# Seven block products in place of eight for the gate and up projections of layer 1

## The chip, the cores and the metric

The kernel runs on one core of one Trainium2 chip. The metric is the time of one execution on the device in microseconds; three executions of the kernel before are known. One execution was also taken by the hardware profiler, and all rows below are from its trace.

## What is computed

The reference is a two-layer backbone over 512 latent tokens of width 1024, with 256 context tokens beside them. Each layer mixes tokens (four groups of heads) and then applies a feed-forward network (FFN) to each token:

```python
def swiglu(h, w_in_, w_out_):
    gate, up = jnp.split(h @ w_in_, 2, axis=-1)
    return (jax.nn.silu(gate) * up) @ w_out_

x = x + g_a * rms_norm(mix_x @ w_out, norm_g[1])
x = x + g_f * rms_norm(swiglu(modulate(rms_norm(x, norm_g[2]), sh_f, sc_f), w_ffn_in, w_ffn_out), norm_g[3])
```

The hidden layer of the FFN has 2816 columns, that is 22 tiles of 128, once for gate and once for up. The second layer, which the code counts as l = 1, has an FFN for the latent tokens only. It is the last thing that the kernel does.

## The kernel before, in words

Every matrix is held transposed: features in the 128 partitions, tokens along the columns. A tile has 128 features, so h (1024 features, 512 tokens) is eight tiles `hf0` to `hf7`. Products are made from float32 numbers that are split into a rounded part `hi` and a remainder `lo`, and each product of tiles is three matmuls (hi by hi, lo by hi, hi by lo; lines 425 to 427). The weights come from DRAM in units of 512 KB (L380, tiles `wr`, four buffers) and are split when they arrive: ACT writes `hi` (L366, tiles `wh`, five buffers of 128x512), and `lo` = source minus `hi` is made on POOL or DVE (L367, tiles `wl`, four buffers). PSUM results of PE are in tiles `mm`, of which there are four.

The end of a layer (`layer_end`) is the output projection, the residual and the norm of the FFN's input (`modnorm`, lines 518 to 533: a product on DVE in L525, `hi` on ACT in L527, `lo` on POOL or DVE), both for one half of the tokens and then for the other, and then `ffn`. In layer 1 `ffn` takes the 22 hidden tiles in three chunks of 8, 7 and 7. The first three tiles run in halves of 256 tokens while the second half's norm is still being made. For each of the other 19 tiles, a unit of gate weights and a unit of up weights arrive, and 48 matmuls of 512 columns (8 tiles of rows, three matmuls each, twice) give two PSUM tiles. `ffn_gate` (lines 1452 to 1460) makes the hidden tile of them:

```python
nc.scalar.activation(a, pg, AF.Tanh)                                                                        # L1456
nc.vector.scalar_tensor_tensor(out=a, in0=a, scalar=1.0, in1=pg, op0=ALU.add, op1=ALU.mult)                  # L1457
nc.vector.tensor_tensor(out=a, in0=pu, in1=a, op=ALU.mult)                                                   # L1458
self.split(g.h[j], g.l[j], a, scale=0.5)   # ACT L369, DVE L370
```

After each chunk come eight output products, one for each tile of features of y, over the chunk's hidden tiles (`ffo`). They are copied or added into y by ACT (L1404) or DVE (L1406). The last chunk's products end in halves, and then the residual is made and stored.

No order is written by hand: the tile framework's scheduler sets it from its own estimates, and each engine then runs its instructions strictly in that order. An instruction that waits for a buffer or an operand therefore holds all that stand behind it on its engine.

## Time and profile before

| | before |
|---|---|
| three executions | 1692.64, 1692.86, 1695.9 us |
| median | 1692.86 us |
| profiled execution: span from first to last instruction | 1692.6 us |
| mean granted TensorE clock in it | 0.972 |
| busy: PE | 1624.3 us (96%) |
| busy: DVE, ACT, POOL | 944.4 us (56%), 740.5 us (44%), 607.2 us (36%) |
| DMA moved | 215.10 MB, 126 GB/s read from HBM over the span |
| chain that ended last | PE 83%, DVE 8%, DMA 3%, ACT 2%, POOL 1% |

PE is TensorE's matmuls, DVE is VectorE, ACT ScalarE, POOL GpSimd and SP the engine that issues the loads. Busy time is the time in which an instruction ran or was held while running; the chain that ended last is the work followed back from the last instruction through whatever released it. The profiled execution's own time is the span, which lies 0.3 us under the median, so a sum made against the profile needs no correction. Layer 1's FFN is the last stage: its norm begins at about 1303 us, its 19 whole hidden tiles and their output products fill the time from about 1346 us on.

### The profile page before, as it was taken

The page shows a single profiled execution, that of the slowest core. Times are in us where ns is not written, and L with a number is a line of the kernel's source. Part 1 is how long each engine was busy: PE and PEld are TensorE (multiplying, and loading weights), DVE is VectorE, ACT ScalarE, POOL GpSimd, SP SyncE. Part 2 cuts the span into 40 slices and gives each one's busy share as a digit, 9 for nine tenths or more (in the row PEclk, how much of TensorE's full clock was granted, in tenths as well). Part 3 has the DMA queues.
Part 4 walks back from the last instruction along what each step waited for, and adds up shares of the span by engine and source line. Part 5 has one row for each costly group of instructions (what it writes and reads, how often), then busy time and mean ns, then how long its engine had stood idle before and what let it go on. Part 6 is the DMA issues. An engine that isn't in the chain of part 4 may idle for free.

```text
span 1692.6 us, 27131 instructions
## 1 busy us (share of the span) xinstructions
PE 1624.3 (96%) x9935; PEld 1381.3 (82%) x9935; DVE 944.4 (56%) x2172; ACT 740.5 (44%) x1658; POOL 607.2 (36%) x691
## 2 busy tenths in 40 slices
PE   6899999999999999999999998999798999999997
PEld 2876778787989998888888888999578988888887
DVE  4876675858685569542443466758765531232344
ACT  3654456654445655333332334465565433332331
POOL 2421333664466565322222225332425322222233
PEclk9999999999999998999999998999799999999998
DMA  9554564254466423334334452122042122323221
GB/s 315 178 181 154 190 222 125 98 176 129 148 230 184 148 74 116 112 138 149 138 127 150 137 201 95 59 73 70 2 132 81 38 93 94 98 82 107 92 95 51
DMA packets 81045, 215.10 MB, mean 127 GB/s; under 512 B 10512, under 2 KB 18576, under 8 KB 80912
## 3 DMA queue, kind: packets, MB, share of 16 engines
q1 hardware_dynamic: 80912, 213.37, 38.3%
q8 instruction: 78, 1.28, 0.3%
q14 instruction: 55, 0.45, 0.1%
HBM read 209.14 MB, written 4.19 MB: 126 GB/s over the span
## 4 chain that ended last, share of the span: by engine, by line
PE 83%; DVE 8%; DMA 3%; issue 2%; ACT 2%; POOL 1%; SPq 0%; DVEq 0%; POOLq 0%; ACTq 0%
PE mm L425 22%; PE mm L427 22%; PE mm L426 22%; PE ms L584 2%; PE mx L1097 2%; PE mm L437 1%; PE mx L1091 1%; PE mm L438 1%; DMA wm_m<-in_wmod_dram 1%; PE mx L1349 1%; PE mm L449 1%; PE mm L443 1%; PE mm L442 1%; PE mm L444 1%; DVE wl L367 1%
## 5 line engine op out<-in xcount | busy, mean ns | idle before, releaser
L366 ACT ACTIVATE wh<-wr 128x512 fp32r<-128x512 f32 (+3 forms) x526 | 318.9, 616 | 581.5 <-PE mm L426 478.9
L367 POOL TENSOR_TENSOR wl<-wr,wh 128x512 fp32r<-128x512 f32 (+2 forms) x248 | 322.8, 1304 | 666.1 <-PE mm L427 517.8
L367 DVE TENSOR_TENSOR wl<-wr,wh 128x512 fp32r<-128x512 f32 (+3 forms) x278 | 206.7, 747 | 180.5 <-PE mm L427 131.5
L425 PE MATMUL mm<-hfh_m,wh 128*128 128x512 f32 (+1 forms) x656 | 253.7, 387 | 0.0
L426 PE MATMUL mm<-hfl_m,wh 128*128 128x512 f32 (+1 forms) x656 | 253.5, 386 | 0.0
L427 PE MATMUL mm<-hfh_m,wl 128*128 128x512 f32 (+1 forms) x656 | 253.4, 386 | 0.0
L425 PEld LDWEIGHTS mm<-hfh_m,wh 128*128 128x128 f32 x656 | 123.7, 188 | 26.5
L427 PEld LDWEIGHTS mm<-hfh_m,wl 128*128 128x128 f32 x656 | 123.5, 188 | 26.5
L426 PEld LDWEIGHTS mm<-hfl_m,wh 128*128 128x128 f32 x656 | 123.5, 188 | 26.5
L425 PE MATMUL mm<-gh_m,wh 128*128 128x512 f32 x275 | 108.3, 394 | 0.0
L426 PE MATMUL mm<-gl_m,wh 128*128 128x512 f32 x275 | 108.1, 394 | 0.0
L427 PE MATMUL mm<-gh_m,wl 128*128 128x512 f32 x275 | 108.0, 393 | 0.0
L1458 DVE TENSOR_TENSOR ft_m<-mm,ft_m 128x512 f32<-128x512 f32 (+1 forms) x50 | 31.3, 626 | 133.2 <-PE mm L427 131.7
L426 PE MATMUL mm<-hfl_c,wh 128*128 128x256 f32 x352 | 100.3, 285 | 1.0 <-POOL hfl_c L532 1.0
L425 PE MATMUL mm<-hfh_c,wh 128*128 128x256 f32 x352 | 99.9, 285 | 0.0
L427 PE MATMUL mm<-hfh_c,wl 128*128 128x256 f32 x352 | 99.2, 283 | 0.0
L627 DVE SCALAR_TENSOR_TENSOR macc_m<-wr,cs,macc_m 128x512 f32<-128x512 f32 x56 | 44.1, 787 | 65.8 <-DMA wr<-in_wmod_dram 64.8
L425 PEld LDWEIGHTS mm<-hfh_c,wh 128*128 128x128 f32 x352 | 66.2, 188 | 4.0 <-issue 3.4
L426 PEld LDWEIGHTS mm<-hfl_c,wh 128*128 128x128 f32 x352 | 66.3, 188 | 2.3 <-POOL hfl_c L532 1.2
L427 PEld LDWEIGHTS mm<-hfh_c,wl 128*128 128x128 f32 x352 | 66.1, 188 | 1.3 <-issue 1.0
L1406 DVE TENSOR_TENSOR y_m<-mm,y_m 128x256 f32<-128x256 f32 (+1 forms) x43 | 23.6, 551 | 68.2 <-PE mm L427 68.2
L427 PEld LDWEIGHTS mm<-gh_m,wl 128*128 128x128 f32 x275 | 51.7, 188 | 12.0
(597 smaller groups left out, 4165.5 us busy)
## 6 DMA issues: line engine op xcount, KB each, us to landing
wr<-in_wfi_dram SPq DMA_DIRECT2D x132, 512.0 KB, 3.6
wr<-in_wmod_dram SPq DMA_DIRECT2D x80, 512.0 KB, 3.6
wr<-in_wT_dram SPq DMA_DIRECT2D x42, 512.0 KB, 3.8
wr<-in_wfo_dram SPq DMA_DIRECT2D x32, 512.0 KB, 3.5
wr<-in_wfo_dram SPq DMA_DIRECT2D x32, 448.0 KB, 3.3
wr<-in_wo_dram SPq DMA_DIRECT2D x24, 512.0 KB, 3.6
wm_m<-in_wmod_dram SPq DMA_DIRECT2D x32, 256.0 KB, 5.3
wr<-in_wRB_dram SPq DMA_DIRECT2D x12, 384.0 KB, 3.3
```

The source lines that it names most:

```text
L366: nc.scalar.activation(hi, src, AF.Copy)
L367: (eng or nc.vector).tensor_tensor(out=lo, in0=src, in1=hi.bitcast(F32), op=ALU.subtract)
L425: nc.tensor.matmul(out, lh, rh, start=first, stop=False)
L426: nc.tensor.matmul(out, lh, rl, start=False, stop=False)
L427: nc.tensor.matmul(out, ll, rh, start=False, stop=last)
L437: nc.tensor.matmul(out, w.h[w0 + i], ah, start=f, stop=False)
L438: nc.tensor.matmul(out, w.l[w0 + i], ah, start=False, stop=False)
L584: nc.tensor.matmul(ps[o:o + 32, :], self.cs[:, k, :], ws[i], start=True, stop=True, tile_position=(0, o))
L627: nc.vector.scalar_tensor_tensor(out=t, in0=w, scalar=self.cs[:, k, s:s + 1], in1=t, op0=ALU.mult, op1=ALU.add)
L1097: nc.tensor.matmul(po[kv * 64:kv * 64 + 64, 0:256], stream.av.t[b][:, kv * 64:kv * 64 + 64], pts[kv].t[:, i * 256:(i + 1) * 256], start=i0 ...
L1406: nc.vector.tensor_tensor(out=yt, in0=ps, in1=yt, op=ALU.add)
L1458: nc.vector.tensor_tensor(out=a, in0=pu, in1=a, op=ALU.mult)
```

## The change

For the 19 whole hidden tiles of layer 1, gate and up are computed as one product of 2x2 blocks in Strassen's form (Winograd's variant). The rows of the pair of block matrices are gate and up, the sum over 1024 features is cut into two halves of four tiles, and the tokens into two halves of 256. The product then takes seven products of blocks and a number of sums in place of eight products of blocks.

- `Quarters` holds h as four blocks `hf00`, `hf01`, `hf10`, `hf11`, and a float32 copy, `keep`. With `keep`, `modnorm` has one more ACT operation for those tiles of features whose `lo` was made on DVE, and `lo` is a plain difference.
- `strassen_rhs` makes four sums of blocks of h, `st0` to `st3`, once: 16 differences on 128x256, 16 `hi` on ACT and 16 `lo`; half of the differences and of the `lo` are on POOL, half on DVE.
- `strassen_pair` replaces the dense products and `ffn_gate` for each of the 19 tiles. It adds four sums of weights (`s[0]` and `s[2]` on POOL, `s[1]` and `s[3]` on DVE, tiles `ws`, four buffers), splits seven blocks of 128x512 (products 0, 3, 4 and 6 with `lo` on POOL, 1, 2 and 5 on DVE), makes 7 x 4 x 3 = 84 matmuls of 256 columns, and takes partial sums out of PSUM between the products.
- The chunks of hidden tiles are 4, 4, 4, 3 and 7 in place of 8, 7 and 7, so there are 40 output products in place of 24 with the same number of matmuls, each with its copy or sum into y, and 40 loads of output weights in place of 24, of the same total size.
- One unit less is loaded ahead for the FFN (`preu1` 3 in place of 4), and the program's scratch for dynamic DMAs is given a size.

```diff
- 'preu1': 4,
+ 'preu1': 3,
...
+ 'strassen': (1,),
+ 'fcs': ((0, 4), (4, 8), (8, 12), (12, 15), (15, 22)),
+ 'sad': 'PPVV',
+ 'slo': 'PVVPPVP',
+ 'sup': 'V',
+ 'sgl': 'V',
+ 'ws': 4}
...
+            if keep is not None:
+                nc.scalar.activation(keep.t[k], tt, AF.Identity, bias=B[:, k:k + 1])
+                self.e(T["mnk"][k]).tensor_tensor(out=lo, in0=keep.t[k], in1=hi.bitcast(F32), op=ALU.subtract)
+            elif T["mnk"][k] == "V":
...
+    def strassen_rhs(self, h):
...
+        sub = lambda c, o, a, b: self.e(c).tensor_tensor(out=o, in0=a, in1=b, op=ALU.subtract)
+        for k in range(nk):
+            x11, x12, x21, x22 = f0[k], f1[k], f0[k + nk], f1[k + nk]
+            sub("V", x11, x12, x11)
+            sub("P", x12, x22, x12)
+            sub("V", x22, x22, x11)
+            sub("P", x21, x21, x22)
+            for t, x, c in ((out[1], x22, "V"), (out[0], x11, "P"), (out[2], x12, "V"), (out[3], x21, "P")):
+                nc.scalar.activation(t.h[k], x, AF.Copy)
+                sub(c, t.l[k], x, t.h[k].bitcast(F32))
...
+        return out, [b11, b21, out[1], out[0], out[2], b22, out[3]]
...
+    def strassen_pair(self, l, j, h, rhs, g, jj):
...
+        a11, a12, a21, a22 = raw[0][:, 0:512], raw[0][:, 512:1024], raw[1][:, 0:512], raw[1][:, 512:1024]
...
+        tt(ad[0], s[0], a21, a22, ALU.add)
+        tt(ad[1], s[2], a11, a21, ALU.subtract)
+        tt(ad[2], s[1], s[0], a11, ALU.subtract)
+        tt(ad[3], s[3], a12, s[1], ALU.subtract)
+        lhs = [a11, a12, s[1], s[0], s[2], s[3], a22]
...
+        for i in range(7):
+            hi = self.wh.tile([P, HALF], F32R, tag="wh", name=self.name("wh"))[:, 0:512]
+            lo = self.wl.tile([P, HALF], F32R, tag="wl", name=self.name("wl"))[:, 0:512]
+            self.split(hi, lo, lhs[i], eng=self.e(T["slo"][i]))
...
+            ps, first = [(z, True), (y, True), (z, False), (w, True), (z, False), (w, False), (z, False)][i]
+            for k in range(KT // 2):
+                c = slice(k * P, k * P + P)
+                self.mac3(ps[:, 0:n], hi[:, c], lo[:, c], rhs[i].h[k], rhs[i].l[k], first and k == 0, k == KT // 2 - 1, not first)
+            if i == 0:
+                nc.scalar.activation(p1, z[:, 0:n], AF.Copy, scale=0.5)
+            elif i == 1:
+                nc.vector.scalar_tensor_tensor(out=c1t[:, 0:n], in0=y[:, 0:n], scalar=0.5, in1=p1, op0=ALU.mult, op1=ALU.add)
+            elif i == 2:
+                nc.scalar.activation(q, z[:, 0:n], AF.Copy, scale=0.5)
+            elif i == 3:
+                nc.scalar.activation(p5t, w[:, 0:n], AF.Copy)
+            elif i == 4:
+                nc.vector.tensor_tensor(out=c2t, in0=z[:, 0:n], in1=p5t, op=ALU.add)
+                p5.free()
+            elif i == 5:
+                nc.vector.scalar_tensor_tensor(out=c1t[:, n:2 * n], in0=w[:, 0:n], scalar=0.5, in1=q, op0=ALU.mult, op1=ALU.add)
+
+        a = e.t[:, 0:2 * n]
+        nc.scalar.activation(a, c1t, AF.Tanh)
+        nc.vector.scalar_tensor_tensor(out=a, in0=a, scalar=1.0, in1=c1t, op0=ALU.add, op1=ALU.mult)
+        nc.vector.tensor_tensor(out=a[:, 0:n], in0=z[:, 0:n], in1=a[:, 0:n], op=ALU.mult)
+        tt(T["sup"], a[:, n:2 * n], a[:, n:2 * n], c2t, ALU.mult)
+        self.split(g.h[jj], g.l[jj], a, eng=self.e(T["sgl"]))
```

Products 0, 2, 4 and 6 all add up in the same PSUM tile `z`, and between them its value is read out: `p1` after product 0 (ACT), `q` after product 2 (ACT), `c2` after product 4 (DVE), each of which must be done before the next of these products may begin. In the listings below, the number at the end of a name tells one tile from another, L403 is the `hi` split and L404 the `lo` split of the changed kernel, and L1538 its plain sums. The scheduler orders PE up to layer 1's output projection as before.

**ACT where the first two whole tiles of a chunk meet.** Before (here the second chunk's first tile, with gate sum `mm_15899`):

```order
L366 ACTIVATE wh_15967<-wr_15965 128x512
L1456 ACTIVATE ft_m_15949<-mm_15899 128x512
L366 ACTIVATE wh_15971<-wr_15965 128x512
L366 ACTIVATE wh_16033<-wr_16031 128x512
L369 ACTIVATE gh_m_15865<-ft_m_15949 128x512
L366 ACTIVATE wh_16037<-wr_16031 128x512
L366 ACTIVATE wh_16043<-wr_16041 128x512
```

And of the change (third chunk, first tile `z` = `mm_16330`, second tile `z` = `mm_16472`; the `wh` rows from `wr_16460` or `ws_1646x` are the second tile's):

```order
L403 ACTIVATE wh_16438<-wr_16320 128x512
L403 ACTIVATE wh_16476<-wr_16460 128x512
L1570 ACTIVATE fd_m_16332<-mm_16390 128x256
L403 ACTIVATE wh_16493<-wr_16460 128x512
L1568 ACTIVATE fe_m_16333<-mm_16330 128x256
L403 ACTIVATE wh_16511<-ws_16465 128x512
L1578 ACTIVATE fe_m_16333<-fc_m_16331 128x512
L403 ACTIVATE wh_16528<-ws_16464 128x512
L403 ACTIVATE wh_16546<-ws_16466 128x512
L1564 ACTIVATE fe_m_16475<-mm_16472 128x256
L403 ACTIVATE wh_16563<-ws_16467 128x512
```

In the order before, ACT has four splits of 128x512, one tanh and one split of the result for each hidden tile. In the changed order it has seven splits, three reads of PSUM, the tanh and the split of the result. The read `p1` of the second tile (L1564, `mm_16472`) stands behind the `hi` of that tile's product 4 (`ws_16466`), and the splits go through five buffers, so each of them waits for the PE work on the fifth one before it.

**PE at the same place** of the change, first around the start of the second tile's product 0 (`st1` is product 2, `hf00` product 0, `hf11` product 5):

```order
L463 MATMUL mm_16330<-st1l_m_15207,wh_16369 128x256
L464 MATMUL mm_16330<-st1h_m_15206,wl_16370 128x256
L462 MATMUL mm_16472<-hf00h_m_14609,wh_16476 128x256
L463 MATMUL mm_16472<-hf00l_m_14610,wh_16476 128x256
L462 MATMUL mm_16390<-hf11h_m_14621,wh_16421 128x256
L463 MATMUL mm_16390<-hf11l_m_14622,wh_16421 128x256
L464 MATMUL mm_16390<-hf11h_m_14621,wl_16422 128x256
```

and then around the start of its product 2 (`st3` is product 6):

```order
L462 MATMUL mm_16330<-st3h_m_15214,wh_16438 128x256
L463 MATMUL mm_16330<-st3l_m_15215,wh_16438 128x256
L464 MATMUL mm_16330<-st3h_m_15214,wl_16439 128x256
L462 MATMUL mm_16472<-st1h_m_15204,wh_16511 128x256
L463 MATMUL mm_16472<-st1l_m_15205,wh_16511 128x256
L464 MATMUL mm_16472<-st1h_m_15204,wl_16512 128x256
```

PE has two matmuls of the second tile's product 0 directly behind product 2 of the first tile, and product 2 of the second tile directly behind product 6 of the first. Product 0 is finished, and products 1 and 3 are done or begun, between these two places.

**DVE and POOL in the middle of the last chunk.** Before, DVE for one and a half hidden tiles (POOL has two rows L367 for each):

```order
L367 TENSOR_TENSOR wl_16038<-wr_16031,wh_16037 128x512
L1457 SCALAR_TENSOR_TENSOR ft_m_16025<-ft_m_16025,mm_15975 128x512
L1458 TENSOR_TENSOR ft_m_16025<-mm_15976,ft_m_16025 128x512
L367 TENSOR_TENSOR wl_16048<-wr_16041,wh_16047 128x512
L370 SCALAR_TENSOR_TENSOR gl_m_15868<-ft_m_16025,gh_m_15867 128x512
L367 TENSOR_TENSOR wl_16114<-wr_16107,wh_16113 128x512
L1457 SCALAR_TENSOR_TENSOR ft_m_16101<-ft_m_16101,mm_16051 128x512
L1458 TENSOR_TENSOR ft_m_16101<-mm_16052,ft_m_16101 128x512
```

And of the change, DVE for one hidden tile (its `z` is `mm_17782`):

```order
L404 TENSOR_TENSOR wl_17874<-ws_17777,wh_17873 128x512
L1538 TENSOR_TENSOR ws_17917<-ws_17916,wr_17912 128x512
L404 TENSOR_TENSOR gl_m_17615<-fe_m_17643,gh_m_17614 128x512
L1538 TENSOR_TENSOR ws_17919<-wr_17912,ws_17917 128x512
L1572 TENSOR_TENSOR fd_m_17784<-mm_17782,fd_m_17784 128x256
L404 TENSOR_TENSOR wl_17946<-wr_17912,wh_17945 128x512
L1575 SCALAR_TENSOR_TENSOR fc_m_17783<-mm_17842,fe_m_17785 128x256
L404 TENSOR_TENSOR wl_17964<-ws_17917,wh_17963 128x512
L1579 SCALAR_TENSOR_TENSOR fe_m_17785<-fe_m_17785,fc_m_17783 128x512
L1580 TENSOR_TENSOR fe_m_17785<-mm_17782,fe_m_17785 128x256
L1538 TENSOR_TENSOR fe_m_17785<-fe_m_17785,fd_m_17784 128x256
```

with POOL for about the same time:

```order
L404 TENSOR_TENSOR wl_17839<-ws_17774,wh_17838 128x512
L1538 TENSOR_TENSOR ws_17916<-wr_17914 128x512
L404 TENSOR_TENSOR wl_17857<-ws_17776,wh_17856 128x512
L1538 TENSOR_TENSOR ws_17918<-wr_17912,wr_17914 128x512
L404 TENSOR_TENSOR wl_17891<-wr_17772,wh_17890 128x512
L404 TENSOR_TENSOR wl_17929<-wr_17912,wh_17928 128x512
```

Before, DVE had two `lo` splits and three operations of the gate for each hidden tile, and POOL two `lo` splits. Now DVE has thirteen operations for each hidden tile, of which `c2` (L1572) stands behind two sums of weights and the `lo` of the gate's result, and POOL has two sums and four `lo` splits.

## Rows read from the trace of the kernel before

**Rows 1.** The page's head and its line of PE and the other engines.
```profile
span 1692.6 us, 27131 instructions
PE 1624.3 (96%) x9935; PEld 1381.3 (82%) x9935; DVE 944.4 (56%) x2172; ACT 740.5 (44%) x1658; POOL 607.2 (36%) x691
```

**Rows 2.** Busy time by stretch: whole hidden tiles, then the norm before them.
```profile
core 0: us, PE busy (x) PEld busy (x) DVE busy (x) ACT busy (x) POOL busy (x), PEclk, DMA share, GB/s
1420.00:1490.00 70.00, 70.00 (x304) 56.77 (x303) 16.77 (x25) 22.71 (x38) 15.56 (x13) 1.00 0.28 91
1300.00:1345.00 45.00, 41.91 (x324) 41.03 (x325) 29.20 (x66) 20.92 (x51) 18.80 (x22) 0.92 0.17 58
```

**Rows 3.** Timeline of ACT: tanh of a whole hidden tile, and of the fifth after it.
```profile
1460.64 0.58 ACT L1456 ACTIVATE ft_m<-mm 128x512 f32<-128x512 f32 x1
...
1516.21 0.58 ACT L1456 ACTIVATE ft_m<-mm 128x512 f32<-128x512 f32 x1
```

**Rows 4.** Timeline of PE: first and last of 73 matmuls of 256 columns.
```profile
1652.67 0.28 PE L427 MATMUL mm<-gh_m,wt_m 128*128 128x256 f32 x1
...
1661.17 0.28 PE L427 MATMUL mm<-gh_m,wt_m 128*128 128x256 f32 x1
```

**Rows 5.** Groups by form, from 1290 us to the end: ACT and DVE.
```profile
L366 ACT ACTIVATE wh<-wr 128x512 fp32r<-128x512 f32 x107 | 67.5, 632 | 181.8 <-PE mm L426 178.8 <-DMA wr<-in_wfi_dram 3.0
L1456 ACT ACTIVATE ft_m<-mm 128x512 f32<-128x512 f32 x19 | 11.0, 580 | 0.0
L1404 ACT ACTIVATE y_m<-mm 128x256 f32<-128x256 f32 x3 | 1.1, 369 | 1.6 <-PE mm L427 1.6
L1406 DVE TENSOR_TENSOR y_m<-mm,y_m 128x512 f32<-128x512 f32 x11 | 7.6, 689 | 32.5 <-PE mm L427 32.5
L1406 DVE TENSOR_TENSOR y_m<-mm,y_m 128x256 f32<-128x256 f32 x10 | 4.2, 420 | 10.3 <-PE mm L427 10.3
```

**Rows 6.** Timeline: a `lo` split on POOL and one on DVE, apart from each other.
```profile
1429.90 1.29 POOL L367 TENSOR_TENSOR wl<-wr,wh 128x512 fp32r<-128x512 f32 x1 [4.26 <-PE mm L427]
...
1432.53 0.69 DVE L367 TENSOR_TENSOR wl<-wr,wh 128x512 fp32r<-128x512 f32 x1 [4.85 <-PE mm L427]
```

**Rows 7.** Timeline of DVE and POOL: sums of squares on both at once.
```profile
41.40 0.69 DVE L479 TENSOR_TENSOR sq_m<-sq_m,sq_m 128x512 f32<-128x512 f32 x1 [1.26 <-ACT sq_m L484]
...
41.97 2.99 POOL L479 TENSOR_TENSOR sq_m<-sq_m,sq_m 128x512 f32<-128x512 f32 x2 [0.54 <-ACT sq_m L484]
...
42.44 3.06 DVE L479 TENSOR_TENSOR sq_m<-sq_m,sq_m 128x512 f32<-128x512 f32 x2 [0.35 <-ACT sq_m L484]
```

**Rows 8.** Timeline of DVE and POOL: pairs of `lo` splits that overlap.
```profile
1290.98 1.22 DVE L367 TENSOR_TENSOR wt_m<-wr,wt_m 128x512 fp32r<-128x512 f32 x1
...
1291.62 1.74 POOL L367 TENSOR_TENSOR wt_m<-wr,wt_m 128x512 fp32r<-128x512 f32 x1
...
1298.32 1.42 POOL L367 TENSOR_TENSOR wt_m<-wr,wt_m 128x512 fp32r<-128x512 f32 x1 [0.61 <-ACT wt_m L366]
...
1298.52 1.77 DVE L367 TENSOR_TENSOR wl<-wr,wh 128x512 fp32r<-128x512 f32 x1
```

**Rows 9.** Timeline: DVE with an operand in PSUM (`mx`) while POOL works.
```profile
1303.85 3.22 DVE L525 SCALAR_TENSOR_TENSOR mn_t<-x_m,Af,mx 128x256 f32<-128x256 f32 x8 [1.35 <-PE mx L515]
...
1305.75 0.74 POOL L532 TENSOR_TENSOR hfl_m<-mn_t,hfh_m 128x256 fp32r<-128x256 f32 x1 [1.26 <-ACT mn_t L531]
```

**Rows 10.** Timeline: the same two engines on 128x256, two operands in SBUF.
```profile
1289.22 1.83 DVE L546 TENSOR_TENSOR x_m<-x_m,rs_t 128x256 f32<-128x256 f32 x2
...
1289.86 0.92 POOL L546 TENSOR_TENSOR x_m<-x_m,rs_t 128x256 f32<-128x256 f32 x1
```

**Rows 11.** Timeline: the second half's norm on ACT, and PE behind it.
```profile
1325.74 0.91 ACT L527 ACTIVATE hfh_m<-mn_t,Bf 128x256 fp32r<-128x256 f32 x2 [2.63 <-DVE mn_t L525]
1326.30 0.38 PE L437 MATMUL mm<-hfh_m,wt_m 128*128 128x256 f32 x1 [0.37 <-ACT hfh_m L527]
```

**Rows 12.** The page's DMA issues: gate and up weights.
```profile
wr<-in_wfi_dram SPq DMA_DIRECT2D x132, 512.0 KB, 3.6
```

More of the change, by code (lines that the diff above doesn't have):

```diff
@@ L1460, in ffn_gate @@
         t.free()
+    def strassen_rhs(self, h):
+        nc = self.nc
+        nk = KT // 2
+        (b11, b12), (b21, b22) = h.blocks
+        f0, f1 = (f.t for f in h.keep)
+        out = [HL(self.ar, f"st{i}", nk, h.half) for i in range(4)]
+        sub = lambda c, o, a, b: self.e(c).tensor_tensor(out=o, in0=a, in1=b, op=ALU.subtract)
[8 more added lines that the diff above has]
+                sub(c, t.l[k], x, t.h[k].bitcast(F32))
+        for f in h.keep:
+            f.free()
+        b12.free()
+        h.blocks = [[b11], [b21, b22]]
+        return out, [b11, b21, out[1], out[0], out[2], b22, out[3]]
@@ L1488, in ffn @@
             while j < j1:
+                if sums:
+                    self.strassen_pair(l, j, h, rhs, g, j - j0)
+                    j += 1
+                    continue
                 wg, wu = self.weights(*win(j, 0)), self.weights(*win(j, 1))
@@ L1497, in ffn @@
                 h.free()
+                for t in sums or []:
+                    t.free()
             if y is None:
@@ L1759, in layer_end @@
         self.ph = 4
-        self.ffn(l, X, h[0], self.mod_col(p, l, 0, "Gf"), T["fcx"], T[f"first{l}"], T[f"hold{l}"], T[f"last{l}"], T[f"hold2{l}"], then, lambda: at(3), ahead if pn else None)
+        self.ffn(l, X, h[0], self.mod_col(p, l, 0, "Gf"), T["fcs" if l in T["strassen"] else "fcx"], T[f"first{l}"], T[f"hold{l}"], T[f"last{l}"], T[f"hold2{l}"], then, lambda: at(3), ahead if pn else None)
 @with_exitstack
```

66 lines of the change are left out of this document (58 added, 8 removed).

## The prediction

> **What bounds the kernel now.** I read the page's head and its line of engines first: PE is busy for 1624.3 of 1692.6 us, the other three for half of the span or less [rows 1]. So what counts is the PE time of a stage, and whether a wait is added there. The busy time by stretch says that in the stage which the change touches PE has no gap: 70.00 of 70.00 us, at a granted clock of 1.00, with DVE at 17, ACT at 23 and POOL at 16 us. In the norm ahead of it PE is busy for 41.91 of 45 us [rows 2]. The timeline of ACT gives the period of a whole hidden tile: five of them between two tanh, (1516.21 − 1460.64)/5 = 11.11 us, which is 48 matmuls of 512 columns at 0.2315 us [rows 3]. The span lies 0.3 us under the median of 1692.86 us, so the sum below is made against the median. A difference under 0.2%, 3.4 us, could not be told from no change.
>
> **What PE gains.** A tile now has 84 matmuls of 256 columns. In this kernel 72 such intervals take 8.50 us, 0.118 us each [rows 4]: a half as wide matmul costs half, 0.116, and hardly anything on top. So 84 × 0.118 = 9.92 us, 1.19 less per tile, and 19 tiles give **−22.7 us** if nothing else limits them. Output products have the same matmuls as before.
>
> **What a tile now asks of the others.** ACT: seven splits of 0.63, a tanh of 0.58, the result's split of 0.63 and three PSUM reads of 0.37 [rows 5] make 6.7 us, under 9.92. POOL: four `lo` and two sums, 6 × 1.29 = 7.7 us [rows 6]. DVE: seven operations of 128x512 with both operands in SBUF (two sums, three `lo`, the gate product of L1579 and the result's `lo`) at 0.69 [rows 6], and five of 128x256 at 0.42, four of which read PSUM [rows 5], make 6.9 us; the rest of its thirteen operations in the order shown is the same work for a neighbouring tile. Each engine alone would fit.
>
> **But DVE and POOL hold each other up.** The trace shows it wherever both work on operands in SBUF. Sums of squares, alone 0.69 on DVE, run on both at once from 42.09 to 45.50: two on each, 1.71 us for a pair, though POOL could do its part in 1.29 [rows 7]. In one pair of splits POOL ends 1.16 us after DVE, and in the other DVE ends 0.55 after POOL [rows 8]: 1.16 + 0.55 = 1.71 again. So of an operation 1.16 on POOL and 0.55 on DVE exclude the other. The DVE operations that read PSUM ran eight in a row in 3.22 us, 0.40 each, with a POOL operation beside them [rows 9]: these I don't count. On 128x256 a pair takes 0.92 [rows 10], and I count half of 0.55, 0.28, for the one such product. A tile then holds the shared way for 6 × 1.16 + 7 × 0.55 + 0.28 = **11.09 us, which is more than PE's 9.92**. Before, a tile had two POOL `lo` and three such DVE operations (two `lo`, the result's): 3.97 us.
>
> 11.09 is the lower bound for a tile in which nothing is ahead; the upper one is the full durations one after the other, 6 × 1.29 + 7 × 0.69 + 0.42 = 12.99. I take 11.72: 11.09 and one `hi` split of 0.63 [rows 5], since once a tile both engines have an operation first in order whose `hi` ACT has only begun. It stays near the lower bound because the pairs in [rows 7, 8] were themselves back to back. How does it reach PE? `c2` stands on DVE behind the result's `lo` and two sums, each of which may first sit out a POOL operation, and product 6 may not begin before `c2` is read; and PE needs each `lo` one product after its `hi`, from rings of four. The surplus of 11.72 over 9.92 is 1.8 us.
>
> The 19 tiles come in runs of 1, 4, 4, 3 and 7. The single tile I count at 9.92. The last tile of the other four has only its own gate work left on DVE and output products next on PE, so I count 0.7 for it (one SBUF operation of DVE, rows above): 2.8 us. The first one has its weights prepared during the output products, but there ACT's order costs twice: the second tile's first `hi` waits for the buffer of product 2, and PE has two matmuls of it directly behind that product; a split of 0.63 and a read of 0.37 later PE goes on. And `p1` stands behind the `hi` of product 4, which waits for the buffer of product 6, while PE has product 2 directly behind 6: again 0.63 + 0.37. With 0.15 for each pair of hand-overs (my choice, under the 0.37 that PE waited for ACT in [rows 11]) it is 2.3 us per run, 9.2 for four. The remaining ten tiles cost 1.8 each, 18.0.
>
> **Ahead of the tiles.** The sums of h are 32 operations of 128x256 on DVE and POOL together, 16 pairs × 0.92 = 14.7 us [rows 10]. They can begin when the second half's norm ends, about 1330 us (its `hi` begin at 1325.74 [rows 11]), and PE wants the first of them about 1346: 1344.7 against 1346, with the first tile's own sums and `lo` on the same way. I take +2, between 0 and 7 (half of the 14.7 uncovered). The norm has four more ACT operations in each half, 0.91/2 = 0.46 each [rows 11]; the first half's lie under the output projection's last products, of the second's I count two: +1.
>
> **At nothing:** the weight loads. A tile's two units of 512 KB, 3.6 us each to landing [rows 12], are wanted every 9.92 or more, with four buffers; 106 GB/s in place of 91 [rows 2]. They wait longer for a buffer, as `a22` is split last; if this cover is gone, PE waits and the chain shows `wr`. Also 16 more output products with 0.69 on DVE [rows 5] in stages of 2.78 (12 matmuls × 0.2315) and more: DVE is idle there. One unit less ahead: two `wr` come during the three halved tiles of over 30 us. The scratch size touches no instruction.
>
> **The sum:** −22.7 + 18.0 + 9.2 + 2.8 + 2 + 1 = +10.3, so **1703 us**. Its own range is 1697 to 1711: middle tiles at 11.09 give 6 less, and at 12.5 give 8 more.
>
> The Trainium skill has a rule that speaks against this change (SBUF — State Buffer, "Who interferes with whom"): DVE and GpSimd share a pair of ports, whoever starts first has it for the whole instruction, and two SBUF inputs on DVE are enough to contend. On that an instruction is excluded for all of its time; the trace agrees that they exclude each other, but 1.71 a pair is less than 1.29 + 0.69 = 1.98.
>
> **Rivals.**
> 1. *The shared way does not bind*: the two engines fall into each other's gaps, and the scheduler runs far enough ahead. PE sets the tile at 9.92, and only ACT's waits and the sums of h remain: −22.7 + 9.2 + 3 = −10.5, **1682 us**; without ACT's waits 1673. For it: 7.7 and 6.9 us are under 9.92, and ACT at 6.7 has room. Against: [rows 7, 8]. It decides where a pair costs under 1.5 us. Chance 0.20.
> 2. *The lead covers half*: during output products POOL and DVE prepare more than one tile, so that of the ten middle tiles half the loss is seen: 9 and 1.4 less, **1693 us**, no change. For it: four buffers of `wl` hold over half a tile. Against: the run of seven is too long for it. Chance 0.18.
> 3. *Whoever starts holds the other off for the whole instruction*: a middle tile takes 12.99, and the ten cost 10 × 3.07 = 30.7 in place of 18.0, the last ones 1.5 each more: **1722 us**. Against: 1.71. By the skill's rule named above it would come out so. Chance 0.09.
>
> That a matmul of 256 columns costs more than half, so that PE would gain nothing, [rows 4] all but exclude.
>
> **How the numbers follow.** The forecast has the remaining 0.53. Faster by over 0.2% is rival 1 and a little of rival 2: 0.25. Within 0.2%: most of rival 2 and the forecast's lowest end: 0.18. Slower: 0.57. The range goes from 1680, which leaves out rival 1 without ACT's waits, to 1719, which leaves out rival 3.
>
> **What would show it.** In the profile after: matmul intervals of 0.118 inside a product; a tile's period, tanh to tanh, of 11.1 to 12.5 us in the run of seven and PE idle by 10 to 20% there, its waits ending on DVE `fd` (`c2`), DVE `wl` or POOL `wl`; POOL's 128x512 mean well above 1.30 us and DVE's above 0.69 us; ACT `wh` and `fe` as releasers once or twice a run. A period near 10 with POOL at 1.30 shows rival 1 and makes the prediction wrong; waits on `wr`, or a lower granted clock in this stage, would be a cause that I have not counted.

## The result, and the profile after

The changed kernel takes 1714.45 us (median of four executions, 1711.73 to 1716.44) beside 1694.01 us for the kernel before: ratio 1.0117, 95% interval 1.0101 to 1.0132. It is slower, as forecast, but by 20.4 us where 10.3 were forecast. The page of the profiled execution begins:

```profile
span 1713.2 us, 29130 instructions
PE 1617.4 (94%) x10619; PEld 1407.8 (82%) x10619; DVE 1100.2 (64%) x2337; ACT 798.2 (47%) x1796; POOL 749.0 (44%) x783
```

PE is busy for 6.9 us less than in [rows 1], yet the span is 20.6 us longer. DVE has 156 us more, POOL 142. Where the time went is read from three places in each trace: the first matmul on the norm's h (1305.42 before, 1308.01 after), the first matmul of the first whole tile (1343.36 before, 1360.52 after) and the end. From the first to the second PE needs 37.94 us before and 52.51 after, **14.6 more**. From there to the end it is 349.2 and 352.7, **3.5 more**. The 2.6 us by which the first place itself differs cannot be put down to the change: over the profiles of this study it lies anywhere between 1301.8 and 1308.0, and the spread is there before the stage begins (the 7001st matmul of the trace begins at 1150.6 us in the change's profile, at 1146.8 before and at 1145.6 in e12). So a difference of a few us between two whole times, medians too, need not come from the edit; below, the profiles are compared from the norm's first `hi` on.

The busy time by stretch, before (head, then whole tiles up to the last tanh):

```profile
core 0: us, PE busy (x) PEld busy (x) DVE busy (x) ACT busy (x) POOL busy (x), PEclk, DMA share, GB/s
1305.42:1343.36 37.94, 37.57 (x306) 37.37 (x307) 24.18 (x55) 17.55 (x44) 15.69 (x19) 0.96 0.07 24
1343.36:1633.00 289.64, 289.64 (x1254) 235.01 (x1253) 76.87 (x117) 91.83 (x155) 70.91 (x55) 1.00 0.30 95
```

and after:

```profile
1308.00:1360.52 52.52, 44.10 (x309) 43.13 (x310) 39.09 (x75) 28.09 (x73) 37.70 (x39) 0.85 0.10 30
1327.00:1333.00 6.00, 5.28 (x25) 5.31 (x26) 2.56 (x8) 0.75 (x2) 0.00 (x0) 0.50 0.00 0
1354.50:1357.00 2.50, 2.50 (x14) 2.50 (x14) 2.15 (x6) 1.65 (x5) 2.50 (x4) 0.50 0.02 7
...
1360.52:1657.00 296.48, 278.93 (x1942) 258.27 (x1941) 224.67 (x266) 139.92 (x266) 190.34 (x129) 0.99 0.31 95
1494.50:1497.00 2.50, 2.50 (x13) 2.50 (x13) 1.76 (x3) 1.00 (x2) 1.67 (x2) 0.50 0.28 93
```

In the head PE has the same work (306 and 309 matmuls), but it stands for 8.4 us where it stood for 0.4, and is busy for 6.5 us more: the granted clock is 0.50 in the windows 1327 to 1333 and 1354.5 to 1357, and 0.85 in the mean where it was 0.96. These two, 8.05 and 6.53, are the 14.6. In the tiles DVE and POOL are now busy or held for three quarters and two thirds of the time, and PE stands for 17.5 us.

**The tiles.** Below are five tanhs of the run of seven (timeline of ACT), then PE's waits from 1357 to 1660 us (total, times, longest), then DVE with PE around one of them, and last two matmuls of PE with 82 intervals between them:

```profile
1600.99 0.63 ACT L1578 ACTIVATE fe_m<-fc_m 128x512 f32<-128x512 f32 x1 [0.43 <-DVE fc_m L1575]
1612.03 0.63 ACT L1578 ACTIVATE fe_m<-fc_m 128x512 f32<-128x512 f32 x1 [1.32 <-DVE fc_m L1575]
1624.88 0.63 ACT L1578 ACTIVATE fe_m<-fc_m 128x512 f32<-128x512 f32 x1 [2.10 <-DVE fc_m L1575]
1635.90 0.63 ACT L1578 ACTIVATE fe_m<-fc_m 128x512 f32<-128x512 f32 x1 [1.31 <-DVE fc_m L1575]
1648.76 0.63 ACT L1578 ACTIVATE fe_m<-fc_m 128x512 f32<-128x512 f32 x1 [2.09 <-DVE fc_m L1575]
```

```profile
PE mm L462 <- DVE fd_m L1572: 12.3, 7, 1.8
PE mm L464 <- POOL wl L404: 4.6, 9, 1.8
PE mm L462 <- ACT fe_m L1564: 0.5, 2, 0.3
```

```profile
1616.68 1.76 DVE L404 TENSOR_TENSOR wl<-ws,wh 128x512 fp32r<-128x512 f32 x1
1618.54 1.61 DVE L1538 TENSOR_TENSOR ws<-ws,wr 128x512 f32<-128x512 f32 x1
1620.07 1.77 DVE L404 TENSOR_TENSOR gl_m<-fe_m,gh_m 128x512 fp32r<-128x512 f32 x1
1621.77 1.75 DVE L1538 TENSOR_TENSOR ws<-wr,ws 128x512 f32<-128x512 f32 x1
1623.44 0.41 DVE L1572 TENSOR_TENSOR fd_m<-mm,fd_m 128x256 f32<-128x256 f32 x1
...
1623.91 0.39 PE L462 MATMUL mm<-st3h_m,wh 128*128 128x256 f32 x1 [1.74 <-DVE fd_m L1572]
```

```profile
1480.83 0.28 PE L463 MATMUL mm<-st3l_m,wh 128*128 128x256 f32 x1
...
1490.55 0.28 PE L464 MATMUL mm<-hf11h_m,wl 128*128 128x256 f32 x1
```

These four periods are 11.04, 12.85, 11.02 and 12.86 us, 11.94 in the mean (11.11 before, [rows 3]). The run's first period is 15.25 us and its last 8.3. The 82 intervals take 9.72 us, 0.1185 each. Four DVE operations in a row take 1.6 to 1.8 us each in place of 0.69 [rows 6], each sitting out one of POOL's; `c2` (`fd`) stands behind them, and product 6 behind `c2`.

**The head.** PE's waits between 1290 and 1370 us (the first of them lies ahead of the first matmul on h):

```profile
PE mm L474 <- ACT hf00h_m L564: 4.9, 1, 4.9
PE ms L541 <- DVE sq_t L516: 4.1, 2, 3.9
PE mm L462 <- DVE ft_m L1497: 2.5, 1, 2.5
PE mm L474 <- ACT hf01h_m L564: 1.2, 1, 1.2
PE mm L486 <- DVE hf10l_m L567: 0.8, 1, 0.8
```

Then the start of the second half's residual on DVE before the change, and rows of the timelines after it: POOL, DVE, ACT, and at last DVE with PE around the wait for `ft`:

```profile
1311.42 3.22 DVE L545 SCALAR_TENSOR_TENSOR rs_t<-y_m,Ga,mx 128x256 f32<-128x256 f32 x8 [2.22 <-PE mx L515]
```

```profile
1315.17 1.28 POOL L1538 TENSOR_TENSOR ws<-wr 128x512 f32<-128x512 f32 x1 [0.83 <-DMA wr<-in_wfi_dram]
1316.41 1.29 POOL L1538 TENSOR_TENSOR ws<-wr,wr 128x512 f32<-128x512 f32 x1
...
1316.49 1.76 DVE L1538 TENSOR_TENSOR ws<-ws,wr 128x512 f32<-128x512 f32 x1 [2.37 <-POOL ws L1538]
1318.17 3.21 DVE L585 SCALAR_TENSOR_TENSOR rs_t<-y_m,Ga,mx 128x256 f32<-128x256 f32 x8
...
1325.80 0.64 ACT L1496 ACTIVATE ft_m<-mm 128x256 f32<-128x256 f32 x2
...
1338.22 0.51 ACT L564 ACTIVATE hf01h_m<-mn_t,Bf 128x256 fp32r<-128x256 f32 x1 [0.17 <-DVE mn_t L562]
...
1351.88 0.94 DVE L1510 TENSOR_TENSOR st2l_m<-hff_m,st2h_m 128x256 fp32r<-128x256 f32 x1
1352.74 0.41 DVE L1497 SCALAR_TENSOR_TENSOR ft_m<-ft_m,mm 128x256 f32<-128x256 f32 x1
...
1353.21 0.38 PE L462 MATMUL mm<-hf01h_m,wh 128*128 128x256 f32 x1 [2.53 <-DVE ft_m L1497]
```

Before, the first gate of the halved tiles (tanh, L1456) began at 1313.53, 9.2 us after the norm's first `hi`, and the second half's first `hi` came 21.4 us after it. Now these are 18.3 and 30.8 us. The copies stand ahead that did not, and so do the sums of weights of the first Strassen tile. DVE waited 2.4 us for POOL's sum, which had itself waited 0.8 us for its load, and came to the second half's residual only after a sum of its own that took 1.76 us beside POOL. The residual began 10.7 us after the norm's first `hi` in place of 7.1; 1.7 us of the 3.7 are that sum, the rest a later `mx` from PE (from 1315.55 on, 8.1 us after the first `hi`, before 6.4). PE's 4.1 us for the second half's norm (`sq_t`) stand behind the residual. PE's 2.5 us for `ft` are another place: a gate of the halved tiles (L1497) that stands on DVE behind sums of h (L1510).

### The profile page after: what moved, and what is told of

The parts are those of the page before. It is cut to its first block, busy times and chain, and to the rows that moved or that the text cites. A ratio compares the mean times of both kernels' runs of the same rounds, so it can differ in the third digit from the quotient of the medians.

```text
span 1713.2 us, 29130 instructions
## 1 busy us (share of the span) xinstructions
PE 1617.4 (94%) x10619; PEld 1407.8 (82%) x10619; DVE 1100.2 (64%) x2337; ACT 798.2 (47%) x1796; POOL 749.0 (44%) x783
## 5 line engine op out<-in xcount | busy, mean ns | idle before, releaser
L404 POOL TENSOR_TENSOR wl<-wr,wh 128x512 fp32r<-128x512 f32 (+2 forms) x248 | 334.6, 1355 | 504.4 <-PE mm L464 304.0
L403 ACT ACTIVATE wh<-wr 128x512 fp32r<-128x512 f32 (+2 forms) x507 | 305.3, 615 | 465.2 <-PE mm L463 330.1
L404 DVE TENSOR_TENSOR wl<-wr,wh 128x512 fp32r<-128x512 f32 (+3 forms) x259 | 202.1, 784 | 89.4 <-ACT wh L403 45.6
L462 PE MATMUL mm<-hfh_m,wh 128*128 128x512 f32 (+1 forms) x320 | 125.3, 391 | 0.0
L463 PE MATMUL mm<-hfl_m,wh 128*128 128x512 f32 (+1 forms) x320 | 125.0, 390 | 0.0
L464 PE MATMUL mm<-hfh_m,wl 128*128 128x512 f32 (+1 forms) x320 | 124.8, 390 | 0.0
L403 ACT ACTIVATE wh<-ws 128x512 fp32r<-128x512 f32 x76 | 46.9, 629 | 56.0 <-PE mm L463 26.9
L464 PEld LDWEIGHTS mm<-hfh_m,wl 128*128 128x128 f32 x320 | 60.5, 189 | 13.5
L462 PEld LDWEIGHTS mm<-hfh_m,wh 128*128 128x128 f32 x320 | 60.5, 189 | 13.4
L463 PEld LDWEIGHTS mm<-hfl_m,wh 128*128 128x128 f32 x320 | 60.4, 189 | 13.1
L404 POOL TENSOR_TENSOR wl<-ws,wh 128x512 fp32r<-128x512 f32 x38 | 55.2, 1463 | 25.0 <-PE mm L464 18.7
L1446 DVE TENSOR_TENSOR y_m<-mm,y_m 128x512 f32<-128x512 f32 (+1 forms) x59 | 33.8, 585 | 50.0 <-PE mm L464 50.0
```

The lines of the kernel that those rows point to most:

```text
L403: nc.scalar.activation(hi, src, AF.Copy)
L404: (eng or nc.vector).tensor_tensor(out=lo, in0=src, in1=hi.bitcast(F32), op=ALU.subtract)
L462: nc.tensor.matmul(out, lh, rh, start=first, stop=False, skip_group_check=more)
L463: nc.tensor.matmul(out, lh, rl, start=False, stop=False, skip_group_check=more)
L464: nc.tensor.matmul(out, ll, rh, start=False, stop=last, skip_group_check=more)
L1446: nc.vector.tensor_tensor(out=yt, in0=ps, in1=yt, op=ALU.add)
```

## The experiments

Two theories were put to the test, one for each place. **S**: in the tiles the shared way of DVE and POOL costs; its rival is the length of the chain in DVE's and ACT's order, whoever shares. **W** (sums of weights), later **Q** (sums of h), **C** (copies) and **G** (the gate alone): ahead of the tiles it is the order in the queues, not the amount of new work. **K**, the rival to W: the new work on h is the cost itself.

**e1: all sums of weights on DVE.**

```diff
- 'sad': 'PPVV',
+ 'sad': 'VVVV',
```

> All four sums of weights of a tile on DVE (sad VVVV), nothing else changed. Shared way (an operation holds it 1.16 us on POOL, 0.55 on DVE): a tile now holds it for 4 x 1.16 + 9 x 0.55 + 0.28 = 9.87 us in place of 11.09, so the mean period of the four middle tiles of the last run falls from 11.94 us to between 10.0 and 10.8, and the whole kernel gains 8 to 15 us on the changed one. Rival, latency (the order of c2 behind DVE's queue and of ACT's buffers sets the period, not the shared way): DVE has two operations of 0.69 more in its queue, so the period stays at 11.9 or grows to 13.

Measured: 1705.23 us, 9.2 under the changed kernel, ratio to before 1.0056 (1.0041 to 1.0071). The gain has S's size, but only 4.3 of the 11.2 us between the two profiles lie behind the first whole tile's tanh; 2.7 are a shorter head and 4.3 an earlier start of the norm. The period is not in S's range: in the run of seven it is 12.53 us in the mean (12.80, 12.37, 12.58, 12.36), the rival's number. The clock has a part in it, 0.50 in the windows 1595.5 to 1598 and 1619.5 to 1622; without that it would be about 11.8 (an estimate: some 16 matmuls each time at 0.213 us in place of 0.118). In the runs of four the first two intervals fell from 13.7 and 12.0 to 12.4 and 11.3, and the last rose from 8.3 and 9.9 to 10.3. PE's waits from 1575 to 1650 us, a row each of POOL and DVE, and DVE a little later without POOL:

```profile
PE mm L462 <- ACT fe_m L1564: 5.5, 2, 2.8
PE mm L462 <- ACT wh L403: 3.5, 3, 2.5
```

```profile
1602.26 3.00 POOL L404 TENSOR_TENSOR wl<-ws,wh 128x512 fp32r<-128x512 f32 x2 [4.18 <-DVE wl L404]
...
1602.32 1.79 DVE L1538 TENSOR_TENSOR ws<-wr 128x512 f32<-128x512 f32 x1
...
1619.06 0.68 DVE L1538 TENSOR_TENSOR ws<-ws,wr 128x512 f32<-128x512 f32 x1
1619.66 0.68 DVE L404 TENSOR_TENSOR gl_m<-fe_m,gh_m 128x512 fp32r<-128x512 f32 x1
```

DVE still sits out POOL's splits, and the wait has moved: `p1` (L1564) now stands on ACT behind the split of the result, which waits for a DVE product that was held up. Adding up how long a tile holds the shared way (9.87 us by S) is no forecast of the period; what stands behind a held operation decides.

**e2: sums and `lo` splits of the tiles all on DVE.**

```diff
+ 'sad': 'VVVV',
+ 'slo': 'VVVVVVV',
```

> All sums of weights and all lo splits of the Strassen tiles on DVE, POOL has nothing in these tiles. Shared way: DVE's operations go back to 0.69 each, 13 x 0.69 + 5 x 0.42 = 11.07 us of DVE work per tile set the period, 11.1 to 11.4 us, a gain of 5 to 10 us on the changed kernel although one engine now does what two did. Latency: 6 more operations in one queue, period 13 or more and slower than the changed kernel.

Measured: 1686.95 us, ratio 0.9953 (0.9937 to 0.9970), 27.5 us under the changed kernel and faster than before. The five periods from the second to the last tanh of the run of seven, 1578.32 to 1628.40, are 10.02 us in the mean: PE's own 9.92. The groups by form from 1575 to 1645 us, first of the changed kernel, then of e2:

```profile
L404 POOL TENSOR_TENSOR wl<-wr,wh 128x512 fp32r<-128x512 f32 x11 | 18.9, 1740 | 0.7 <-PE mm L464 0.7
L404 DVE TENSOR_TENSOR wl<-ws,wh 128x512 fp32r<-128x512 f32 x12 | 15.6, 1302 | 0.0
L1538 DVE TENSOR_TENSOR ws<-ws,wr 128x512 f32<-128x512 f32 x7 | 10.2, 1458 | 1.8 <-POOL ws L1538 1.5
```

```profile
L404 DVE TENSOR_TENSOR wl<-ws,wh 128x512 fp32r<-128x512 f32 x20 | 13.6, 682 | 0.5 <-ACT fe_m L1578 0.2 <-PE mm L464 0.2
L1538 DVE TENSOR_TENSOR ws<-ws,wr 128x512 f32<-128x512 f32 x4 | 2.7, 678 | 0.0
```

DVE's split goes from 1302 to 682 ns and its sum from 1458 to 678. One engine does what two did, in less time, with a longer queue: the rival (13 us or more) falls, and dividing the work between DVE and POOL is shown to be the cost. For 12.3 of PE's 17.4 us of waits in the tiles this is the shared way, as `c2` stands behind held DVE operations (rows above); the 4.6 for POOL's own `wl` go in e2 too, and whether there POOL's holding or its slower work counted is not separated. From the first whole tile's tanh to the end e2 takes 21.1 us less than the change; the rest of the 27.5 are 2.8 in the head and an earlier start of the norm. S's own number for e2, 11.1, was too high as well. It added durations of 0.69 and 0.42; operations back to back follow each other faster (see the end).

**e3: the first Strassen tile's sums of weights held back.**

```diff
+        if j == T[f"first{l}"]:
+            for i in (0, 2):
+                nc.scalar.activation(s[i][:, 0:1], h.blocks[1][1].h[3][:, 0:1].bitcast(F32), AF.Copy)
         tt(ad[0], s[0], a21, a22, ALU.add)
```

> Two ACT copies of one column make the first Strassen tile's sums of weights wait for the last tile of the second half's norm; all else as in the changed kernel. Theory W (the 17 us ahead of the tiles come mostly from these sums, which stand on DVE and POOL before the second half's residual and wait there for a load): the second half's first hi comes 5 to 9 us earlier than at 1338.2, the interval of half clock after 1326 us goes, and the kernel takes 1703 to 1709 us. Rival K (the copies of h on ACT and the sums of h are the cost themselves): within 2 us of the changed kernel.

Measured: 1708.31 us (1.0078, 1.0063 to 1.0093). The second half's first `hi` comes 24.2 us after the first one in place of 30.8, as W says, but the first whole tile's tanh only 60.2 us after it in place of 61.3. The half clock does not go either: the granted clock is 0.50 in the windows 1321 to 1323.5 and 1342 to 1347. The sums of weights do hold up the second half, and what is won there is lost again before the tiles: most of W's 6 us in the total are a start of the norm that was 5.2 us earlier in this profile. W does not explain the head.

**e4: the head of the change with eight block products.** The norm's copies and the sums of h are made, the sums are not used, and gate and up are products of 256 columns over all of h.

```diff
-                    sums, rhs = self.strassen_rhs(h)
+                    for t in self.strassen_rhs(h)[0]:
+                        t.free()
...
+                    for ps, w in ((pg, wg), (pu, wu)):
+                        for t0 in (0, n // 2):
+                            self.dense(ps[:, t0:t0 + n // 2], w, h, t0, n // 2)
```

> The changed norm with its copies and the sums of h stay, but the sums are not used: gate and up of the 19 tiles are made as eight block products (96 matmuls of 256 columns, 11.33 us a tile by 0.118 each, 4.2 us more in all than 48 of 512), in the three chunks of before. Theory W: the first whole tile starts 3 to 7 us later than the 1343.4 of before, and the kernel takes 1701 to 1706 us. Rival K: it starts at 1355 to 1361, and the kernel takes 1710 to 1716 us.

Measured: 1712.43 us (1.0102, 1.0085 to 1.0119): the rival's number, without any sum of weights. PE waited 10.7 us in one piece for `ft` (L1497), the first gate, which stood on DVE behind the second half's norm and sums of h. From this came theory Q.

**e5 to e8: the sums of h left out, or late.** e5 leaves them out of e4, e6 makes them in e4 after the halved tiles' last gate. e7 does that in e2, e8 in the changed kernel, both with the first whole tile as eight block products so that the sums lie under it. The core of the edit in e6 to e8 (`z` is that gate's result times zero):

```diff
+        nc.vector.tensor_scalar(out=z, in0=g.h[2][:, NX - 1:NX].bitcast(F32), scalar1=0.0, scalar2=1.0, op0=ALU.mult, op1=ALU.mult)
+        for k in range(KT // 2):
+            nc.scalar.activation(h.keep[1].t[k][:, 0:1], h.keep[1].t[k][:, 0:1], AF.Identity, bias=z)
```

> As e4_heads_dense (changed norm with its copies, eight block products of 256 columns), but the sums of h are left out, which nothing uses there. Theory Q (the 17 us are the sums of h standing on DVE ahead of the gate of the halved tiles, so that PE finds no free PSUM tile): the first whole tile's tanh comes 46 to 51 us after the first hi of the norm (45.1 before, 62.4 in e4_heads_dense), the interval of half clock at 1320 to 1337 us goes, and the kernel takes 1699 to 1704 us. Rival K (the copies and the quartering of h are the cost): 58 to 62 us after the first hi, and 1709 to 1714 us.

> As e4_heads_dense, with the sums of h made, but only after the last gate of the halved tiles (one column of four copies gets a zero added that comes from that gate's result). Theory Q, the place in the queue counts: within 2 us of e5_copies_no_sums. Rival (the sums' sheer work on DVE, POOL and ACT counts): within 2 us of e4_heads_dense, 1712.

> As e2_all_on_dve, with the sums of h made after the last gate of the halved tiles, and the first whole tile as eight block products (1.4 us more), under which they lie. Theory Q: the head is 9 to 13 us shorter, so 1674 to 1680 us, faster than both kernels. Rival: the sums only move their cost to the next tile, 1686 to 1690 us.

> The changed kernel with the same late sums of h and the same first whole tile as eight block products; sums of weights and lo splits on POOL and DVE as in the change. Theory Q: 9 to 12 us under the changed kernel's 1714, 1701 to 1706 us, and the periods of the last run as there (11.0 and 12.9 in turn). Rival: within 2 us of 1714.

Measured: e5 1709.53 us (1.0080, 1.0064 to 1.0096), e6 1710.19 (1.0086, 1.0061 to 1.0110), e7 1683.08 (0.9922, 0.9906 to 0.9938), e8 1705.66 (1.0055, 1.0039 to 1.0071). e5 and e6 agree with each other, as Q says, but at the rival's level: without the sums PE still waits 8.0 us for the first gate. e8 gains 8.8 us on the changed kernel and lies in Q's range for the time, e7 only 3.9 on e2 and misses it; e8's profile owes 5.1 to an earlier start of the norm. The last run's periods in e8 are those of the change (11.03, 12.86, 11.03, 12.85), as expected. So the sums of h are part of it and not the whole.

**e9: only the five chunks, in the kernel before.**

```diff
- 'strassen': (1,),
+ 'strassen': (),
...
+        self.ffn(l, X, h[0], self.mod_col(p, l, 0, "Gf"), T["fcs" if l == 1 else "fcx"], T[f"first{l}"], T[f"hold{l}"], T[f"last{l}"], T[f"hold2{l}"], then, lambda: at(3), ahead if pn else None)
```

> The kernel before in all but the chunks of hidden tiles: 4, 4, 4, 3 and 7 in place of 8, 7 and 7 (dense products, norm without copies; one unit less loaded ahead, as in the change). As in the prediction, 16 more output products cost nothing: within 2 us of the kernel before. Rival (each further chunk ends in a wait for the gate's result or a smaller load): 1 to 2 us for each of two more chunks, 1696 to 1700 us.

Measured: 1695.01 us, ratio 1.000 (0.999 to 1.001). The 16 further output products, with one unit less loaded ahead, cost nothing beyond the interval's 1.7 us.

**e10 and e11: no copies, or late ones.** e10 leaves the copies out of e5. e11 is e7 with the copies made late, as `hi` plus `lo` on DVE; the cut shown is common to both.

```diff
-                self.modnorm(X, h[0], A, B, t0, n, h[0].keep[t0 // n])
+                self.modnorm(X, h[0], A, B, t0, n)
```

> As e5_copies_no_sums, without the float32 copies of h (the norm's own operations are those of the kernel before; h stays in blocks, products of 256 columns). Theory C (the copies stand between the hi of a half on ACT, so PE gets eight hi in 7.9 us in place of 4.2, the first gate comes later, and then stands behind the second half's norm): the first whole tile's tanh comes 45 to 48 us after the first hi, the 8.0 us wait for the gate goes, and the kernel takes 1697 to 1701 us. Rival (blocks or the unit less that is loaded ahead are the cost): 56 to 60 us after the first hi, 1707 to 1711 us.

> As e7_all_dve_sums_late, with the copies of h made late too, on DVE, as hi plus lo after the last gate of the halved tiles. Theory C: the first whole tile's tanh comes 45 to 48 us after the first hi in place of 50.5, and the kernel takes 1677 to 1681 us. Rival: 16 more operations on DVE (16 x 0.36 = 5.8 us) push the first Strassen tile back by as much, 1683 to 1688 us.

Measured: e10 1709.68 us (1.0082, 1.0066 to 1.0098), e11 1684.11 (0.9929, 0.9912 to 0.9947). In e10 the first whole tile's tanh is still 58.8 us after the first `hi`: copies are not what the loss needs. In e11 the head is as short as theory C says, 47.1 us, and the total as the rival says. Side by side, in us after the norm's first `hi`, the last column from the first whole tile's tanh:

| | first gate's tanh | second half's first `hi` | first whole tile's tanh | from there to the end |
|---|---|---|---|---|
| before | 9.2 | 21.4 | 45.1 | 343.1 |
| e9, five chunks | 9.1 | 21.3 | 45.0 | 343.5 |
| e11, copies and sums late, all on DVE | 11.7 | 23.1 | 47.1 | 333.8 |
| e7, sums late, all on DVE | 14.8 | 24.3 | 50.5 | 326.7 |
| e8, sums late | 15.0 | 24.4 | 50.7 | 348.6 |
| e2, all on DVE | 17.4 | 27.5 | 58.5 | 323.4 |
| e3, sums of weights late | 14.7 | 24.2 | 60.2 | 343.5 |
| the change | 18.3 | 30.8 | 61.3 | 344.5 |
| e5, no sums | 27.1 | 20.7 | 58.8 | 345.5 |
| e10, no copies, no sums | 27.0 | 22.6 | 58.8 | 345.5 |
| e4, sums, dense | 27.3 | 20.9 | 62.4 | 345.3 |

(A Strassen tile has its tanh some 2 us later in the tile than a dense one: 8.2 us after its first matmul in the change, 6.1 before. That concerns the change, e2 and e3 here.) The scheduler sets the gate's place anew with every edit, and the long heads go with a late gate, or, in e3 and the change, with sums of h ahead of the halved tiles' later gates. No edit so far had moved the gate alone.

**e13: the gate alone, in the kernel before.**

```diff
+        if behind is not None:
+            self.nc.scalar.activation(a[:, 0:1], behind.bitcast(F32), AF.Copy)
...
+                        self.ffn_gate(g, i // 2, *pair, t0, n // 2, h.h[KT - 1][:, n - 1:n] if l == 1 and t0 == 0 else None)
```

> The kernel before with one thing changed: the gates of the halved tiles' first half of tokens wait for the last hi of the second half's norm (one column of their result tile is first written from it), which is the order that e4, e5, e6 and e10 have. Theory G (in the head the place of these gates behind the second half's norm is what costs: PE has filled the four PSUM tiles and stands): first gate 26 to 28 us after the first hi in place of 9.2, the first whole tile's tanh at 56 to 61 us in place of 45.1, an interval of half clock there, 1705 to 1711 us. Rival (blocks of h and 256-column products are needed for the loss): head within 3 us of 45.1, 1694 to 1698 us.

Measured: 1705.07 us, ratio 1.0060 (1.0037 to 1.0083), 10.0 us over the kernel before. Timeline of ACT, PE's wait and the clock:

```profile
1306.26 0.91 ACT L527 ACTIVATE hfh_m<-mn_t,Bf 128x256 fp32r<-128x256 f32 x2 [0.89 <-DVE mn_t L525]
...
1329.64 0.63 ACT L1458 ACTIVATE ft_m<-mm 128x256 f32<-128x256 f32 x2
```

```profile
PE mm L425 <- DVE ft_m L1459: 6.6, 1, 6.6
```

```profile
1325.00:1334.00 9.00, 3.49 (x16) 3.49 (x17) 6.52 (x16) 6.02 (x19) 2.92 (x4) 0.50 0.00 0
```

The gate comes 23.4 us after the first `hi`, PE has filled the four PSUM tiles and stands for 6.6 us, the clock is at half in that stretch, and the first whole tile's tanh is at 54.8 us, 9.7 later than before. Theory G is shown, its time in the range expected and its head a little below: this order alone, without copies, blocks or sums, costs 10 us. It is the order of e4, e5, e6 and e10. The change does not have it: there the first gate, at 18.3, comes ahead of the second half's first `hi`, at 30.8.

**e12 and e14: do head and tiles add up, and what beats both.** e12 is e11 with the change's own engines in the tiles. e14 is e11 with the sums of h on DVE too.

```diff
-            sub("P", x12, x22, x12)
+            sub("V", x12, x22, x12)
...
-            sub("P", x21, x21, x22)
+            sub("V", x21, x21, x22)
-            for t, x, c in ((out[1], x22, "V"), (out[0], x11, "P"), (out[2], x12, "V"), (out[3], x21, "P")):
+            for t, x, c in ((out[1], x22, "V"), (out[0], x11, "V"), (out[2], x12, "V"), (out[3], x21, "V")):
```

> As e11_copies_late (late copies and sums, first whole tile as eight block products), but with the change's own choice of engines in the tiles (PPVV and PVVPPVP). If head and engines add up: head about 47 us as in e11, the last run's periods 11.0 and 12.9 in turn as in the change, 1699 to 1704 us. If the engines' contention is only a consequence of the late head: 1684 to 1690.

> As e11_copies_late, with the sums of h and their lo all on DVE. In e11 the ones on both engines took 0.88 to 0.95 us a pair on 128x256 and DVE alone 0.36, and PE waited 2.9 us for a read of PSUM that stood behind, with half clock after it. Shared way: DVE is through by about 1363 in place of 1367, that wait and the half clock go, 1677 to 1681 us. Rival (DVE's amount of work counts, not the sharing): the wait stays or grows, 1683 to 1687 us.

Measured: e12 1706.06 us (1.0070, 1.0045 to 1.0096), **e14 1680.60 us (0.9917, 0.9901 to 0.9933)**, 14.5 under the 1695.05 of the kernel before beside it. e12 has e11's head (47.1) and the change's periods (11.04, 12.86, 11.01, 12.85), and lies 22 us over e11; its time is 2 us above the range for adding up and 16 above the other. From the first whole tile's tanh to the end the tiles' engines cost 21.4 us with a short head (355.2 against 333.8) and 21.1 with a long one (the change against e2): head and tiles add up. The short head is worth less than it looks. From the change to e12 it is 14.2 shorter, but 10.7 are lost behind it; from e2 to e11 it is 11.4 shorter, and 10.4 are lost (2 of them the later tanh, 1.4 the tile of eight products, the rest late copies and sums). The whole times differ by 8.4 and 2.8, which includes 4.7 and 1.8 us of earlier start of the norm. With the sums alone late, e7 and e8 lose 3.3 and 4.1 behind it, hardly more than the 3.4 of tanh and eight products: for the sums the order counts. The copies, late and on DVE, lose some 7 us more behind the head (e11 against e7) and save 3.4 in it: for them the amount counts too. Part of that rest may be sharing again: with the sums of h on DVE, e14 is 3.5 under e11, though the intervals of the two ratios overlap. In the profiles PE's longest wait in this place falls from 2.9 to 1.7 us, and the half clock behind it is shorter and not gone, as it was expected to be; the stretch from the first whole tile's tanh to the next is 38.9 us in place of 41.6. Two stretches of e14, the run of seven and the head:

```profile
1575.00:1645.00 70.00, 69.40 (x528) 66.45 (x528) 57.81 (x103) 40.59 (x77) 8.38 (x7) 1.00 0.30 97
1304.50:1345.00 40.50, 38.85 (x308) 38.46 (x309) 25.19 (x59) 20.09 (x49) 18.51 (x22) 0.94 0.13 43
```

## Where the prediction was right and where it was wrong

- **PE's gain**, −22.7: right. Interval for interval, 84 of 0.118 us took the place of 48 of 0.2315, and where little holds PE up (e2, e14) the period is 10.0 us.
- **Tiles.** The place was right (`c2` behind the result's `lo` and two sums, each sitting out a POOL operation), and the period, 11.72, measured 11.94. The price of ACT's order at the start of a run, 9.2 in all, was not: PE waited 0.5 us for `p1`. It waits for `c2` there as well, and all waits in the tiles come to 17.4 us where 30 were forecast. Not counted was the clock, at 0.50 from 1494.5 to 1497 and from 1590 to 1592.5, each time behind a wait of 1.8 us, some 3 us in all (about 16 matmuls each time at 0.213 us in place of 0.118); and 5 to 6 us more, an estimate, lie in PE's slow start behind each wait (the interval behind the wait that ended at 1480.61 was 0.22, and the one with the wait of 1.71 in it 1.98). All in all the tiles and what follows cost 3.5 us, forecast 7.3. That the sum came so near is in part luck: 12.6 us too much of waits against some 9 us that had no term. The forecast also counted thirteen DVE operations to a tile, as the text ahead of it does; the code has twelve, those that were priced.
- **Ahead of the tiles: the step that failed.** "+2" for the sums of h and "+1" for the copies counted operations against free time, and PE as wanting only the first whole tile at about 1346. It measured +14.6: 8.05 of standing and 6.53 of busy time at a lower clock. The sums of h and the copies are in queues with the second half's norm and the halved tiles' gates, and the gates are what gives PE its PSUM tiles back. The order of the changed kernel, which was known, has the sums of weights before the second half's residual and the sums of h among the later gates; no term priced these places. The trace of the change shows both: 4.1 us of PE's standing end on the second half's norm, behind the residual that a sum of weights held up by 1.7 us, and 2.5 on a gate behind sums of h. That the new work in the head is the cause, e12 shows: with copies and sums made late and the first whole tile dense, and the change's own engines, the head is 47.1 us, 2.0 over that before. e13 shows the same kind of cost from a gate, 10.0 us with the clock at half behind the wait, in an order that the change itself does not have. How the 14.6 divide between copies, sums of weights and sums of h is not settled: e3 and e8 take parts away, and each makes the scheduler set a new order.
- **At nothing:** the five chunks (e9) were right. The loads were right in the tiles, where PE never waited for `wr`; in the head POOL's first sum of weights waited 0.8 us for one.
- **Rivals.** The shared way binds (e2 against the change), so rival 1 did not happen. That e2's 1686.95 comes near rival 1's 1682 is no sign for its terms: e2 has none of its 9.2 for ACT's order (PE waited 0.8 us for `p1`), and a head 13.4 us longer than before (2 of them the later tanh) where rival 1 counted 3. For rival 2 the lead was too short: the first periods of a run are the longest, 13.7 in the runs of four and 15.25 in that of seven. Rival 3's lock for whole instructions was priced by durations, 12.99 a tile, and 11.94 was measured. But DVE's operations of 128x512 begin 0.60 us apart when they have the way alone, and POOL's two sums at 1315.17 and 1316.41, while DVE stood, 1.24; with 0.33 for the product of 128x256 the lock gives 6 × 1.24 + 7 × 0.60 + 0.33 = 11.97. So the period does not decide against rival 3's mechanism, only against its price. What is left against it is the pair: 1.69 us in the rows around 1618 (the four DVE operations end 5.08 us apart, first to last, in three pairs) where 1.24 + 0.60 = 1.84 would be expected. In e1's rows DVE ends 0.55 us after POOL (1602.32 + 1.79 = 1604.11; POOL's two end at 1605.26, the first of them about 1603.56). The rule named from the Trainium skill (SBUF — State Buffer, "Who interferes with whom") agrees with the trace in who excludes whom; in how long, the whole instruction, it is too strict by 0.15 us a pair.
